# Order of the long and short products with standing weights in a hybrid layer, one Trainium2 core

## The chip, the core and the metric

The kernel runs on one core of one Trainium2 chip, in one launch. The metric is the device time of an execution in microseconds. The program was run three times: 1918.36, 1925.76 and 1926.24 us, so the median is 1925.76 us. Beside these times there is a profile of one execution, taken by the hardware profiler; all rows shown here are from it. Times in the timeline count from the first instruction of the profiled execution.

## The reference, cut to what matters

One layer of a network on 256 tokens of 2048 features, all in fp32. It has a dilated attention of three groups with 8 heads, a gated linear attention with 4 heads, a gated sum of the two branches, an output product, a layer norm, a feed-forward with a short convolution along the tokens, and a second layer norm. What fills the time are the products of the tokens with large weights:

```
parts = split(x @ w_in)            # 2048 x 19472
... attention on parts[:9] ...     # ya = attention @ w_proj_a   (1024 x 2048)
yb = (o * silu(gr)) @ w_proj_b     # 2048 x 2048
y  = sigmoid(m_a) * ya + sigmoid(m_b) * yb
x  = layernorm(ALPHA * x + y @ w_out)              # 2048 x 2048
g, u = x @ w_gate, x @ w_up                        # 2048 x 5632 each
x  = layernorm(ALPHA * x + (silu(conv(g)) * u) @ w_down)   # 5632 x 2048
```

## The kernel before

**Two parts of each number.** Every operand of the large products is split exactly into a main part and a rest of fewer bits each (`split`: ACT copies the number rounded into the main part, DVE subtracts it from the number and leaves the rest). A product is then the sum of main x main, main x rest and rest x main. For the tokens the two parts lie side by side in one tile of 512 columns: 256 tokens' main parts in the first half (`:S`), their rests in the second (`S:`).

**Pieces of weights.** All weights come as pieces of 128 x 2048 numbers, 1 MB each, in the order in which they are used. `piece` loads the next one (SP's queue, line 147), ACT makes the main part `whi` (line 115) and DVE the rest `wlo` (line 116). There are three buffers for the raw piece, two for `whi` and two for `wlo`.

**Two forms of product.** In the form that the diff touches the weights stand in TensorE's array and the tokens move past them; the result is 128 features by tokens. `b_tile` takes for each of 16 steps `kc` of 128 input features (8 steps for `yp`) a main part of the weights, 128 x 128, and moves all 512 columns past it (line 187: the long product), and then the rest of the weights and moves the 256 main columns past it, into the second half of the same bank (line 188: the short product). The first half of the bank then holds main x main, the second half the two mixed products; `b_sum` (lines 231 and 232, ACT and DVE) adds the halves. A bank is one tile of the pool `psm`, which has four.

In the other form (`a_chunk`, `a_part`, lines 237 to 239) the tokens stand and 512 columns of weights move: three products of 512 columns for each 128 tokens and step. It is used for `v`, `gv` and the product with `w_down` (`wd`), and the diff does not touch it.

**Where the touched form is used.** `b16` is `b_tile` with one piece and 16 steps. In order of time: `qk` (48 tiles, in four rounds with a head pair's attention beside them), `gqk` (16), `yp` (16 tiles of 8 steps), `gr` (16), `m` and `pb` (for each of 16 feature tiles two of `m` and one of `pb`), `wo` (16), and in the feed-forward `fg` and `fu` for 44 feature tiles in parts of 20, 20 and 4 (`FSPLIT`). After each part comes `wd`. The operand is `X` (the tokens) up to `m`, `YA` for `yp`, `OB` for `pb`, `YH` for `wo`, `X1` for the feed-forward. `OB` and `YH` are made feature tile by feature tile from the products just before: the last tile of `YH` comes from the last `pb` tile through ACT and DVE, and `wo`'s first tile reads it in its 16th step.

**Three tiles side by side.** The feed-forward's first three tiles (`fg` 0, `fu` 0, `fg` 1) are made by `b16_three` (lines 196 to 211) while DVE and ACT still make `X1` from the layer norm (lines 711 to 715): in each step a long and a short product for each of the three.

**What sets the order.** The kernel is written against a framework that plans each engine's order from dependencies and estimated costs, in the program's order where nothing speaks against it; small jobs of the attention are put into the stream of tiles from a list (`pump`). Each engine then runs its instructions strictly in the planned order. DVE and ACT thus make the split of a coming piece, the sums of a finished tile and the attention's steps one after the other. `piece_in_blocks` makes a piece out of turn, in small blocks.

Of the kernel before, what the change touches and what calls it, by code (L numbers as in the profile page):

```python
# [18 lines left out]
S = 256  # L19
# [13 lines left out]
ALPHA = 2.0 ** 0.25  # L33
# [3 lines left out]

# columns of w_in
C_GQ = 9216
# [6 lines left out]

# columns of the packed per-partition parameters
P_GB = 0
# [9 lines left out]
def hybrid_layer(ctx: ExitStack, tc: tile.TileContext, wp, xt, wgl, gw, par, relb, onehot, ln2, out):  # L58
    nc = tc.nc
# [10 lines left out]
    def act_set(name, after):  # L70
        """Load a set of ACT's tables once the instruction has been issued."""
        with tc.issue_after(after.ins):
            nc.scalar.preload_act_table_set(name)
# [5 lines left out]
    def blk(name, dt=F32):  # L79
        """2 KB of every partition."""  # L80
        n_blk[0] += 1
        return bpool.tile([P, 512], dt, tag="blk", name=f"{name}_{n_blk[0]}", bufs=NBLK)

    def tmp(name, dt=F32):
        """1 KB of every partition."""
        n_blk[0] += 1
        return tpool.tile([P, S], dt, tag="tmp", name=f"{name}_{n_blk[0]}", bufs=NTMP)

    def big(name, shape, dt=F32):
        """3 KB of every partition."""  # L90
        n_blk[0] += 1
        return tpool.tile([P, *shape], dt, tag="big", name=f"{name}_{n_blk[0]}", bufs=7)
# [17 lines left out]

# [1 line left out]
    n_piece = [0]  # L112
# [5 lines left out]
    def piece_in_blocks(i, on_pool=None):  # L118
        """A piece out of turn, or one that leaves the pool's parts to the next."""
        ws = []  # L120
        if on_pool is not None:
            raws = wpool.tile([P, 2048], F32, tag="raw", name=f"raw_{i}", bufs=3)
            nc.sync.dma_start(raws, wp[i])
        for c in range(4):
            cols = slice(c * 512, (c + 1) * 512)
            if on_pool is None:
                raw = blk("braw")
                nc.sync.dma_start(raw, wp[i, :, cols])
            else:
                raw = raws[:, cols]  # L130
            ws.append((blk("bhi", F32R), blk("blo", F32R)))
            split(*ws[-1], raw, nc.gpsimd if c in (on_pool or ()) else nc.vector)
        return ws

    def piece(before=(None,)):
        """Next piece, in as many cuts as there are entries of things to do before a cut."""
        i = n_piece[0]
        n_piece[0] += 1
        raw = wpool.tile([P, 2048], F32, tag="raw", name=f"raw_{i}", bufs=3)
        hi = wpool.tile([P, 2048], F32R, tag="whi", name=f"whi_{i}")  # L140
        lo = wpool.tile([P, 2048], F32R, tag="wlo", name=f"wlo_{i}")
        n = 2048 // len(before)
        for k, f in enumerate(before):
            if f is not None:
                f()
            c = slice(k * n, (k + 1) * n)
            nc.sync.dma_start(raw[:, c], wp[i, :, c])
            split(hi[:, c], lo[:, c], raw[:, c])
        return hi, lo

    side = []
# [9 lines left out]

# [1 line left out]
    def xtiles(name):  # L163
# [15 lines left out]

# [1 line left out]
    def b_tile(name, parts, opnd, nk):  # L181
        """[128 features, tokens]: main part in columns :S, the rest in S:."""
        ps = mbank(name)
        for kc in range(nk):
            hi, lo = parts(kc)
            xo = opnd(kc)
            nc.tensor.matmul(ps, hi, xo, start=(kc == 0), stop=False)  # L187
            nc.tensor.matmul(ps[:, S:], lo, xo[:, :S], start=False, stop=(kc == nk - 1))  # L188
        return ps
# [6 lines left out]
    def b16_three(names, opnd, second):  # L196
        """Three feature tiles side by side, for an operand that is still being made."""
        by_cols = lambda hi, lo: lambda kc: [a[:, kc * P : (kc + 1) * P] for a in (hi, lo)]
        ws = [by_cols(*piece((None,) * 4))]
        by_blk = lambda b: lambda kc: [a[:, (kc % 4) * P : (kc % 4 + 1) * P] for a in b[kc // 4]]  # L200
        ws.append(by_blk(second))
        ws.append(by_blk(piece_in_blocks(n_piece[0] + 1, (0, 1))))
        n_piece[0] += 2
        pss = [mbank(n) for n in names]
        for kc in range(16):
            xo = opnd(kc)
            for w, ps in zip(ws, pss):
                h, l = w(kc)
                nc.tensor.matmul(ps, h, xo, start=(kc == 0), stop=False)
                nc.tensor.matmul(ps[:, S:], l, xo[:, :S], start=False, stop=(kc == 15))  # L210
        return pss
# [4 lines left out]
    def evacuate(name, pss, parts=False):  # L216
        """[tile of tokens], or [tile of tokens][part]"""
        out = []
        for ps in pss:
            if parts:  # L220
                two = blk(name, F32R), blk(name, F32R)
                split(*two, ps)
                out.append(two)
            else:
                out.append(blk(name))
                nc.scalar.activation(out[-1], ps, AF.Copy)
        return out
# [13 lines left out]
    def a_chunk(name, opnd, nk, first=None, n_pump=1):  # L241
        """[128 tokens, 512] for both halves of the tokens."""
        pss = [mbank(f"{name}_t{t}") for t in range(2)]
# [10 lines left out]
    def a_pair_by_half(name, opnd, second):  # L254
        """Two chunks of one piece each: first all of one half of the tokens."""
        hi, lo = piece()
# [11 lines left out]

# [1 line left out]
    ident = cpool.tile([P, P], F32, name="ident")  # L270
# [14 lines left out]

# [1 line left out]
    bvs = dpool.tile([NH, 3, 384], F32, name="bvs")  # L287
# [16 lines left out]
    def copies():  # L304
        """Every row once for each of 32 queries, so that a row's start can move with the query."""
        nc.sync.dma_start(bvd, bvs[:, :, None, :].to_broadcast([NH, 3, 32, 384]))

    side.extend([lambda: None] * 4 + [distances(g) for g in range(3)] + [copies])

# [1 line left out]
    scale = HD ** -0.5  # L311
    YA = [None] * NH

    def attend(h, qk, vs, hp, hv):
        """Stages of head h: hp its place in its q and k tiles, hv in its v tiles."""
        st = {}
# [102 lines left out]

# [1 line left out]
    GK, GQ, GV = [], [], []  # L421
# [9 lines left out]

    # low-rank gate
    glr = tmp("glr")
# [3 lines left out]
    split(glh, gll, glr)  # L437
    # both operands of the gate's product three times over, from rows 0, 32 and 64, so that
    # one pass over the rows sums the products of their parts
    places = [slice(r, r + RANK) for r in (0, 32, 64)]  # L440
# [30 lines left out]
    def gla(h):  # L471
# [33 lines left out]
        def keys():  # L505
            q, k = GQ[h], GK[h]
            e1, e2, e3 = st["e1"], st["e2"], st["e3"]
            nc.vector.scalar_tensor_tensor(q, q, 256.0 ** -0.5, e1, op0=ALU.mult, op1=ALU.mult)
            # groups of two chunks of keys, for the chunks of queries 0 | 1 | 2, 3 | 2 | 3
            xk = [big("xk", (2, 3, 2, CH)) for _ in range(2)]  # L510
# [77 lines left out]

# [1 line left out]
    YP = []  # L590
# [12 lines left out]

# [1 line left out]
    OB = []  # L605
# [12 lines left out]

# [1 line left out]
    YH = []  # L620
# [21 lines left out]

# [1 line left out]
    act_set(ACT_LN_EXP, gated)  # L644
# [6 lines left out]
    def residual(d):  # L651
        """ALPHA x, less the centre."""
        if d % 2 == 0:
            R.append(blk("r"))
        xo = xop(d)
        r = r_of(d)
        nc.gpsimd.tensor_tensor(r, xo[:, :S].bitcast(F32), xo[:, S:].bitcast(F32), op=ALU.add)
        if d:
            nc.vector.scalar_tensor_tensor(r, r, ALPHA, cen, op0=ALU.mult, op1=ALU.subtract)
# [58 lines left out]

# [1 line left out]
    ACC = [[blk("acc") for _ in range(4)] for _ in range(2)]  # L720
# [12 lines left out]

# [1 line left out]
    G2, B2 = [], []  # L735
# [82 lines left out]

# [1 line left out]
def _by_rows(w, c, n):  # L820
    """Columns c..c+n of all rows, 128 rows to a partition's place."""
    k = w.shape[0] // P
# [45 lines left out]
def _bucket_rows():  # L868
    """One-hot buckets of the distance 255 - j, by group; a last row of -1e30 where it is masked."""
    out = np.zeros((NBUCKET + 1, 3, 384), np.float32)  # L870
# [61 lines left out]
```

## Time and profile before

| | |
|---|---|
| median of three runs | 1925.76 us (1918.36 to 1926.24) |
| profiled execution, span from first to last instruction | 1924.5 us |
| PE busy | 1897.7 us, 99% |
| weight loads (PEld) busy, beside PE | 1622.0 us, 84% |
| DVE busy | 1154.3 us, 60% |
| ACT busy | 900.1 us, 47% |
| POOL busy | 104.4 us, 5% |
| moved by DMA | 352.60 MB, mean 183 GB/s |

The span is 1.3 us below the median of the runs. PE stands for the products and PEld for the loads of their weights, which run beside products. The ends of products are modelled and products overlap, so the busy time of PE says that it was never long without work, and not that it worked at its peak. DVE, ACT and POOL are the vector, scalar and general engines, SP issues the transfers.

### The profile page before, as it was taken

Reading aid. Unit: us, or ns where it says so; the run is one execution under the profiler, and the core shown is the slowest. Engines: PE = TensorE matmul, PEld = TensorE weight load, DVE = VectorE, ACT = ScalarE, POOL = GpSimd, SP = SyncE. Lnnn points to the kernel's source line nnn. Section 1 sums busy time; section 2 is a strip of 40 time slices with the busy share of each in tenths; the row PEclk is TensorE's granted clock in tenths of the full one; section 3 lists DMA queues with packets and bytes.
Section 4 is the critical chain, followed back from the end, with each engine's and each line's share of the span. In section 5 each row is a group of like instructions: output and inputs, shape, how many; then the busy total and the mean of one; then the engine's idle time right before and its main releaser. Section 6 shows DMA issues by size and latency. Waiting matters only on the chain.

```text
span 1924.5 us, 24582 instructions
## 1 busy us (share of the span) xinstructions
PE 1897.7 (99%) x10208; PEld 1622.0 (84%) x10208; DVE 1154.3 (60%) x1324; ACT 900.1 (47%) x1084; POOL 104.4 (5%) x130
## 2 busy tenths in 40 slices
PE   9999999999999999999999998999999999999997
PEld 6888888888878888888888887888888888888885
DVE  5466565755656556655555757666654566664557
ACT  5445444453445554544444545554533455544342
POOL 0000000001000000000000452000000000000001
PEclk9999999999999999999999999999999999999998
DMA  7645545455544355555555553455555645555552
GB/s 273 231 178 175 191 175 182 166 191 175 180 154 145 140 191 182 194 178 195 177 193 179 197 192 114 176 190 182 190 186 195 239 180 192 181 191 200 198 194 86
DMA packets 56058, 352.60 MB, mean 183 GB/s; under 512 B 6737, under 2 KB 7660, under 8 KB 15500
## 3 DMA queue, kind: packets, MB, share of 16 engines
q1 hardware_dynamic: 53340, 345.10, 50.0%
q0 software_dynamic: 2464, 5.69, 1.0%
q8 instruction: 80, 1.31, 0.3%
q10 hardware_dynamic: 144, 0.26, 0.0%
q14 instruction: 30, 0.25, 0.0%
HBM read 348.85 MB, written 3.31 MB: 183 GB/s over the span
## 4 chain that ended last, share of the span: by engine, by line
PE 95%; DVE 3%; ACT 1%; issue 1%; DMA 1%; SPq 0%; DVEq 0%; ACTq 0%
PE qk L187 9%; PE fu L187 8%; PE fg L187 8%; PE m L187 6%; PE qk L188 5%; PE fu L188 4%; PE fg L188 4%; PE wd_t L238 4%; PE wd_t L237 4%; PE wd_t L239 4%; PE m L188 3%; PE pb L187 3%; PE gr L187 3%; PE gqk L187 3%; PE wo L187 2%; PE v_t L237 2%
## 5 line engine op out<-in xcount | busy, mean ns | idle before, releaser
L116 DVE TENSOR_TENSOR wlo<-raw,whi 128x2048 fp32r<-128x2048 f32 (+1 forms) x339 | 740.8, 2188 | 597.9 <-ACT whi L115 597.6
L115 ACT ACTIVATE whi<-raw 128x2048 fp32r<-128x2048 f32 (+1 forms) x339 | 617.4, 1824 | 454.7 <-issue 114.0
L187 PE MATMUL qk<-x,whi 128*128 128x512 f32 x768 | 273.8, 400 | 0.0
L187 PE MATMUL fu<-x,whi 128*128 128x512 f32 x688 | 244.9, 398 | 0.0
L187 PE MATMUL fg<-x,whi 128*128 128x512 f32 x672 | 239.7, 399 | 0.0
L188 PE MATMUL qk<-x,wlo 128*128 128x256 f32 x768 | 215.7, 281 | 0.0
L188 PE MATMUL fu<-x,wlo 128*128 128x256 f32 x688 | 193.2, 281 | 0.0
L188 PE MATMUL fg<-x,wlo 128*128 128x256 f32 x672 | 188.7, 281 | 0.0
L187 PE MATMUL m<-x,whi 128*128 128x512 f32 x512 | 181.7, 399 | 0.0
L187 PEld LDWEIGHTS qk<-x,whi 128*128 128x128 f32 x768 | 144.3, 188 | 35.3
L187 PEld LDWEIGHTS fu<-x,whi 128*128 128x128 f32 x688 | 129.2, 188 | 32.1
L187 PEld LDWEIGHTS fg<-x,whi 128*128 128x128 f32 x672 | 126.3, 188 | 31.0
L188 PEld LDWEIGHTS qk<-x,wlo 128*128 128x128 f32 x768 | 145.1, 189 | 0.0
L188 PE MATMUL m<-x,wlo 128*128 128x256 f32 x512 | 143.8, 281 | 0.0
L238 PE MATMUL wd_t<-wlo,h 128*128 128x512 f32 x344 | 134.1, 390 | 0.0
L239 PE MATMUL wd_t<-whi,h 128*128 128x512 f32 x344 | 133.9, 389 | 0.0
L237 PE MATMUL wd_t<-whi,h 128*128 128x512 f32 x344 | 133.7, 389 | 0.0
L188 PEld LDWEIGHTS fu<-x,wlo 128*128 128x128 f32 x688 | 130.0, 189 | 0.0
L188 PEld LDWEIGHTS fg<-x,wlo 128*128 128x128 f32 x672 | 127.0, 189 | 0.1
L187 PEld LDWEIGHTS m<-x,whi 128*128 128x128 f32 x512 | 96.2, 188 | 24.1
L188 PEld LDWEIGHTS m<-x,wlo 128*128 128x128 f32 x512 | 96.7, 189 | 0.0
L187 PE MATMUL pb<-ob,whi 128*128 128x512 f32 x256 | 91.1, 398 | 0.0
(251 smaller groups left out, 2991.5 us busy)
## 6 DMA issues: line engine op xcount, KB each, us to landing
raw<-in_wp SPq DMA_DIRECT2D x316, 1024.0 KB, 4.8
raw<-in_wp SPq DMA_DIRECT2D x24, 256.0 KB, 5.1
bias<-bvd POOLq DMA_DIRECT2D x32, 96.0 KB, 2.7
xraw<-in_xt SPq DMA_DIRECT2D x8, 256.0 KB, 5.2
braw<-in_wp SPq DMA_DIRECT2D x8, 256.0 KB, 5.0
ln<-in_ln POOLq DMA_DIRECT2D x8, 256.0 KB, 5.0
out<-acc SPq DMA_DIRECT2D x7, 256.0 KB, 2.5
bvd<-bvs SPq DMA_DIRECT2D x1, 1152.0 KB
```

The lines of the kernel that those rows point to most:

```text
L115: nc.scalar.activation(hi, src, AF.Copy)
L116: engine.tensor_tensor(lo, src, hi.bitcast(F32), op=ALU.subtract)
L187: nc.tensor.matmul(ps, hi, xo, start=(kc == 0), stop=False)
L188: nc.tensor.matmul(ps[:, S:], lo, xo[:, :S], start=False, stop=(kc == nk - 1))
L237: nc.tensor.matmul(ps, xh, hi, start=first, stop=False)
L238: nc.tensor.matmul(ps, xh, lo, start=False, stop=False)
L239: nc.tensor.matmul(ps, xl, hi, start=False, stop=last)
```

## The change

In `b_tile` the loop over the steps becomes two loops over the same steps: first all long products of the tile, then all short ones. The first product still opens the bank (`start`) and the last short one closes it (`stop`). In `b16_three` the loop over the steps issues the long products of the three tiles, and then come the 16 short ones of each tile in turn. Comments and docstrings are emptied as well, which changes no instruction.

```diff
     def b_tile(name, parts, opnd, nk):
         ps = mbank(name)
         for kc in range(nk):
-            hi, lo = parts(kc)
-            xo = opnd(kc)
-            nc.tensor.matmul(ps, hi, xo, start=(kc == 0), stop=False)
-            nc.tensor.matmul(ps[:, S:], lo, xo[:, :S], start=False, stop=(kc == nk - 1))
+            nc.tensor.matmul(ps, parts(kc)[0], opnd(kc), start=(kc == 0), stop=False)
+        for kc in range(nk):
+            nc.tensor.matmul(ps[:, S:], parts(kc)[1], opnd(kc)[:, :S], start=False, stop=(kc == nk - 1))
         return ps
...
         pss = [mbank(n) for n in names]
         for kc in range(16):
-            xo = opnd(kc)
             for w, ps in zip(ws, pss):
-                h, l = w(kc)
-                nc.tensor.matmul(ps, h, xo, start=(kc == 0), stop=False)
-                nc.tensor.matmul(ps[:, S:], l, xo[:, :S], start=False, stop=(kc == 15))
+                nc.tensor.matmul(ps, w(kc)[0], opnd(kc), start=(kc == 0), stop=False)
+        for w, ps in zip(ws, pss):
+            for kc in range(16):
+                nc.tensor.matmul(ps[:, S:], w(kc)[1], opnd(kc)[:, :S], start=False, stop=(kc == 15))
         return pss
```

## Rows read from the trace of the kernel before

**Rows 1.** Page: busy us (share of the span) by engine, and the chain's shares
```profile
PE 1897.7 (99%) x10208; PEld 1622.0 (84%) x10208; DVE 1154.3 (60%) x1324; ACT 900.1 (47%) x1084; POOL 104.4 (5%) x130
...
PE 95%; DVE 3%; ACT 1%; issue 1%; DMA 1%; SPq 0%; DVEq 0%; ACTq 0%
```
**Rows 2.** Groups by line, forms apart: count | busy us, mean ns | idle before
```profile
L187 PE MATMUL qk<-x,whi 128*128 128x512 f32 x768 | 273.8, 400 | 0.0
```
**Rows 3.** Timeline, PE, feed-forward: start us, duration us, line, product
```profile
1699.79 0.40 PE L187 MATMUL fg<-x,whi 128*128 128x512 f32 x1
1700.02 0.28 PE L188 MATMUL fg<-x,wlo 128*128 128x256 f32 x1
1700.14 0.40 PE L187 MATMUL fg<-x,whi 128*128 128x512 f32 x1
...
1700.50 0.40 PE L187 MATMUL fg<-x,whi 128*128 128x512 f32 x1
...
1705.44 0.40 PE L187 MATMUL fu<-x,whi 128*128 128x512 f32 x1
```
**Rows 4.** Timeline, PE: first products of gr, wo, second part's fg, wd
```profile
702.15 0.40 PE L187 MATMUL gr<-x,whi 128*128 128x512 f32 x1
...
1063.96 0.40 PE L187 MATMUL wo<-yh,whi 128*128 128x512 f32 x1
...
1507.59 0.39 PE L187 MATMUL fg<-x,whi 128*128 128x512 f32 x1
...
1733.71 0.40 PE L237 MATMUL wd_t<-whi,h 128*128 128x512 f32 x1
```
**Rows 5.** Timeline, PE, wd: a long product and the third one after it
```profile
1769.78 0.39 PE L237 MATMUL wd_t<-whi,h 128*128 128x512 f32 x1
...
1770.46 0.39 PE L237 MATMUL wd_t<-whi,h 128*128 128x512 f32 x1
```
**Rows 6.** Timeline, PE, wo: a long product and the 16th long after it
```profile
1077.55 0.39 PE L187 MATMUL wo<-yh,whi 128*128 128x512 f32 x1
...
1083.10 0.39 PE L187 MATMUL wo<-yh,whi 128*128 128x512 f32 x1
```
**Rows 7.** Timeline, PE and PEld, one of the attention's po products
```profile
211.87 0.28 PE L373 MATMUL po<-pT,v 128*128 128x256 f32 x1
211.87 0.19 PEld L374 LDWEIGHTS po<-pT,v 128*128 128x128 f32 x1
211.99 0.28 PE L374 MATMUL po<-pT,v 128*128 128x256 f32 x1
...
212.11 0.23 PE L375 MATMUL po<-pT,v 128*128 128x128 f32 x1
...
212.46 0.28 PE L188 MATMUL qk<-x,wlo 128*128 128x256 f32 x1
```
**Rows 8.** Tile po, PE: duration ns min/median/max, first and last start us
```profile
L374 PE MATMUL po<-pT,v x24: 279/282/285, 212.0 to 533.3; 128*128 128x256 f32 x24
```
**Rows 9.** Timeline, PE, wo near 1104; stretch: busy (x) per engine, PEclk, DMA, GB/s
```profile
1103.55 0.39 PE L187 MATMUL wo<-yh,whi 128*128 128x512 f32 x1
1106.40 0.41 PE L188 MATMUL wo<-yh,wlo 128*128 128x256 f32 x1 [2.46 <-DVE wlo L116]
...
1106.70:1110.00 3.30, 3.30 (x12) 2.82 (x12) 3.27 (x4) 0.42 (x1) 2.05 (x1) 0.50 0.72 253
```
**Rows 10.** Timeline, all engines, end of wo's first tile
```profile
1069.21 0.42 DVE L116 TENSOR_TENSOR yh<-y,yh 128x256 fp32r<-128x256 f32 x1
...
1070.14 0.40 PE L187 MATMUL wo<-yh,whi 128*128 128x512 f32 x1
```
**Rows 11.** Timeline, all engines, the three tiles side by side
```profile
1168.33 0.77 PE L209 MATMUL fg<-x,whi 128*128 128x512 f32 x1 [4.09 <-DVE x L715]
...
1179.91 1.26 DVE L715 SCALAR_TENSOR_TENSOR x<-r,prm,x 128x256 fp32r<-128x256 f32 x3
...
1186.39 0.28 PE L210 MATMUL fg<-x,blo 128*128 128x256 f32 x1
```

## The prediction

> **What bounds the kernel now.** I read the page's busy shares and its chain of waits first. The reader is to see that TensorE is busy for 1897.7 us of a 1924.5 us span and that 95% of the chain that ended last is PE [rows 1]. So every nanosecond that a product takes less time comes off the end, and what ACT, DVE and the DMA queues do counts only where PE waits for them.
>
> Next I read the groups by line. There are two kinds of product: a long one (line 187, 512 columns, weights `whi`) and a short one (line 188, 256 columns, weights `wlo`), 768 of each for `qk` alone. A long lasts 400 ns in the mean [rows 2], but that is not what it costs, because products overlap. The cost is the distance from one start to the next, and that is in the timeline. In the feed-forward the sequence runs long 1699.79, short 1700.02, long 1700.14, and the 17th long, which opens the next tile, is at 1705.44 [rows 3]: one tile of 16 pairs takes 5.65 us, a pair 353 ns. Two longer stretches agree: the 64 tiles of `gr`, `m` and `pb` take 1063.96 - 702.15 = 361.81 us, 5.653 each, and the 40 tiles of the second feed-forward part 1733.71 - 1507.59 = 226.12 us, 5.653 each [rows 4].
>
> Three more places price the same products in other surroundings.
> - In `wd` every product is long and each has its own weights: three take 1770.46 - 1769.78 = 0.68 us, 227 ns each [rows 5]. That is a long after a long.
> - In `wo` the same alternating pairs run at 5.55 us a tile (1083.10 - 1077.55), 347 ns a pair [rows 6]. The alternation has a quick and a slow form, 6.7 ns a pair apart.
> - In the attention's `po` a long product is followed by two of 256 columns and one of 128, each with weights of its own, and then by the next tile's pairs. The first short starts at 211.87, the second at 211.99, the third at 212.11, and the short of the next pair at 212.46 [rows 7]. Two shorts one behind the other: 120 ns. All four slots to 212.46 take 590 ns, which is 3 x 120 + 227 + 3, so even the 128-column one costs no more and no less than 120. The second short's weights begin to load as the first short starts (both at 211.87): the whole load lies beside one short product. Over 24 such places the second short's duration stays between 279 and 285 ns [rows 8].
>
> So 227 + 120 = 347 is the quick pair, and the slow pair has 6.7 ns more. I put those at the long that follows a short: its row reads 0.40 us in the slow tile and 0.39 in the quick one [rows 3, 6], while the short behind a short shows no such spread [rows 8].
>
> **The change part by part.** No product, load, byte or copy is added or removed. Only the order on PE changes: 16 longs, then 16 shorts.
>
> 1. *The slots.* A tile after the change has 15 longs behind a long, one long behind a short, 16 shorts: 16 x 226.7 + 16 x 120 + 7 = 5.554 us, against 5.653: 0.099 us less. Of the kernel's 237 tiles of 16 pairs (`yp`'s 16 half tiles counted as 8), I take as slow the 64 and 40 of [rows 4], the 8 of the last feed-forward part, 37 of the first, 48 `qk`, 8 `yp`, half of the 16 `gqk`: 213. 213 x 0.099 = 21.1 us. The 24 quick ones lose 0.007 each, and a few tiles of the first feed-forward part are quick too: in all -20.3 us. The bounds are from the price of a short in a run of 16, which no row shows beyond three: 120 ns [rows 7] and, at the dear end, 133, which is 120 and what the dearest slow pair has more than the quick one (1700.50 - 1700.14 = 360 against 347 ns [rows 3, 6]). I take 120, since the run of three is the nearest row.
>
> 2. *Waits of ACT and DVE for PE.* The last long of a tile comes 16 x 0.12 = 1.9 us earlier in its tile, so ACT may begin to overwrite `whi` for the piece after next that much sooner, and DVE's `wlo` is wanted only 16 x 0.227 = 3.6 us after a tile begins. Both add slack where PE hardly waits now, so I cost it at nothing. Evacuation (line 231) still waits for the last product of the bank; that comes no later relative to the tile's end.
>
> 3. *A wait that goes.* At 1103.55 a `wo` tile issued its first long and the short behind it waited 2.46 us for DVE's `wlo` [rows 9]. Then the granted clock was 0.50 from 1106.7 to 1110.0, the lower level of 1.2 GHz, after PE had stood still [rows 9]. With 16 longs in front, 3.6 us of work cover the wait: -2.5 us, and half of 3.3 us for the clock: -1.7. Late next is nothing in that tile.
>
> 4. *A wait that comes.* The first `wo` tile is the place where the operand is made just ahead of its use: the rest of `yh` for the 16th step is split by DVE from 1069.21 for 0.42 us, and the next tile's first long is at 1070.14 [rows 10]. Now that step comes at 15 x 353 ns = 5.3 us after 1063.96 and fits. Afterwards the 16th long is due at 1063.96 + 15 x 0.227 = 1067.4 and waits until 1069.63; behind it queue all 16 shorts. 1069.63 + 0.227 + 1.92 = 1071.8 against 1070.14: +1.6 us. If the clock falls behind this wait as it did in [rows 9], another 1.7.
>
> 5. *The three tiles side by side* (`b16_three`) start while DVE still makes `x1`: the first long at 1168.33, the last three parts of the operand from 1179.91 for 1.26 us, the last short at 1186.39 [rows 11]. Now the shorts fill the time between operands. Afterwards 48 longs go first at the operand's pace, and 48 x 0.12 = 5.76 us of shorts come behind: last operand 1181.17, three longs 0.68, shorts 5.76, so 1187.6 at the earliest and 1188.4 if PE is three operands behind. Against 1186.51: +1.1 to +1.9; I take +1.5.
>
> The sum: -20.3 - 4.2 + 1.6 + 1.5 = -21.4 us; 1924.5 - 21.4 = 1903.1 us of span. The median of the runs, 1925.76, lies 1.3 above that span, so 1904.
>
> The Trainium skill's "TensorE: Matmul & The Clock Gate", in the sections "Back-to-back issue gap" and "LDWEIGHTS (loading the stationary operand)", speaks against step 1: it gives a product N/2.4 + 2.5 ns (109 for 256 columns, 216 for 512) and a load of 128 columns 107 ns, so a load always hides and order would not matter; by it step 1 is zero. The trace doesn't agree in size: 227 ns where the page has 216 [rows 5], and an alternating pair that costs 353 in one place and 347 in another [rows 3, 6].
>
> **The rivals.**
> - *Order makes no difference.* The 6.7 ns may belong not to the change of kind but to whatever state PE is in over a long stretch (`wo` ran quick in the same order as `fg` [rows 3, 6]), and would then come back in the run of shorts, 126.7 ns each. For it: the two forms exist without any difference in the program. Against: the 24 tight durations [rows 8], measured amid slow tiles. Step 1 is then about +2 (the quick tiles join the slow), and the rest -1.1: 1925.
> - *The run of shorts is bound by its weight loads: slower.* In the old order every second load has a 227 ns product to lie beside; in the run each has 120. If the delay of a dear pair, 13 ns, falls on each short, a tile takes 16 x 226.7 + 16 x 133.3 = 5.76 us: +0.107 x 213 + 0.21 x 24 = +28 us, with the rest 1953. It decides from 126.7 ns a short upward. A load that could not overlap at all, 188 ns as PEld rows last, would give 16 x 0.068 = 1.1 us a tile; the second load at 211.87 with its product at 211.99 [rows 7] excludes that.
> - *The waits are dearer than I think.* The planner orders the engines anew; if a dozen tiles open a wait of 2 us as in step 4, the gain is gone. For it: step 4 itself. Against: everywhere else the operand is made long before. 1915 to 1925.
>
> **How the numbers follow.** My forecast has 0.64: 1904, by itself 1897 to 1912 (steps 3 to 5 at their ends, and the runs shown differ by 8 us). Order without effect 0.16, dearer waits 0.08, slower 0.12. Faster by over 0.5% (9.6 us, about what a measurement of this kernel can tell from no change) is 0.64 and half of the dear waits' case: 0.68. Within it: 0.16 and the other half, 0.20. Slower: 0.12. For 8 in 10 the range must take in the case without effect: 1896 to 1928.
>
> **What would show it.** In the timeline of the changed kernel a tile would be 16 longs 227 ns apart and then 16 shorts 120 apart, and a tile of the feed-forward 5.55 us. Shorts 127 apart mean the first rival, 130 and over the second. The 2.46 us wait of line 188's kind for `wlo` would be gone, a wait of PE for `yh` of some 2 us would stand in the first `wo` tile, and the three tiles side by side would end 1 to 2 us later after their start. If longs in a run are not 227 apart, or PE shows more than a handful of new waits of a microsecond, the prediction is wrong.

## The result and the profile after

The changed kernel takes 1904.99 us (median of four runs, 1903.91 to 1905.38). The kernel before, run beside it, has 1922.06 us (four runs, 1917.02 to 1926.24). The ratio is 0.9918, with a 95% interval of 0.9895 to 0.9941: faster, by 0.6 to 1.05%. The forecast was 1904, and later the same kernel had 1904.93 (four runs) against 1918.47 (seven runs of before on one chip, 1915.06 to 1923.57), ratio 0.9930 (0.9912 to 0.9948). So the time after the change met the forecast, and the gain, 17.1 us by the first medians and 13.5 by the second, is smaller than the 21 that the forecast took off. The runs of the changed kernel lie within 1.5 us, those of before within 11. That difference in spread belongs to the explanation.

On the page of the changed kernel (busy us by engine, then the chain that ended last) the reader is to see that nothing has changed places: PE still makes 95% of the chain, as in [rows 1]. The profiled execution's span is 1902.1 us, 22.4 below the one of before.

```profile
PE 1878.5 (99%) x10208; PEld 1625.5 (85%) x10208; DVE 1152.7 (61%) x1324; ACT 911.8 (48%) x1084; POOL 86.9 (5%) x130
...
PE 95%; DVE 3%; ACT 1%; issue 1%; DMA 0%; SPq 0%; DVEq 0%; ACTq 0%
```

The timeline of PE in the second feed-forward part answers to [rows 3] (start us, time from the first start to the last end, and how many neighbours a row joins). Line 185 is now the long product, line 187 the short one.

```profile
1489.78 3.79 PE L185 MATMUL fg<-x,whi 128*128 128x512 f32 x16
1493.40 2.08 PE L187 MATMUL fg<-x,wlo 128*128 128x256 f32 x16
1495.32 3.82 PE L185 MATMUL fu<-x,whi 128*128 128x512 f32 x16
1498.97 2.08 PE L187 MATMUL fu<-x,wlo 128*128 128x256 f32 x16
1500.88 1.32 PE L185 MATMUL fg<-x,whi 128*128 128x512 f32 x5
```

A tile takes 1500.88 - 1495.32 = 5.56 us where it took 5.65. The 16 shorts take 1.91 to 1.92 us, 120 ns each. The 16 longs of the first tile, which come behind the long products of `wd`, take 3.62 us, 226 each; those of the second tile, which come behind shorts, take 3.65.

By stages, from the first products of each (they answer to [rows 4] and to the end of `wo`):

```profile
695.98 0.40 PE L185 MATMUL gr<-x,whi 128*128 128x512 f32 x1
...
785.04 0.40 PE L185 MATMUL m<-x,whi 128*128 128x512 f32 x1
...
1142.29 0.38 PE L690 MATMUL pln<-s,ones 128*128 128x256 f32 x1
...
1712.42 0.40 PE L236 MATMUL wd_t<-whi,h 128*128 128x512 f32 x1
```

With `wo`'s first long at 1052.24 (below), `gr`, `m` and `pb` take 356.26 us for 64 tiles, 5.567 each, against 5.653; the 40 tiles of the second feed-forward part 1712.42 - 1489.78 = 222.64, 5.566 each. The `wo` stage, up to the product behind its last tile, takes 1142.29 - 1052.24 = 90.05 us against 93.80 (1157.76 - 1063.96, with this row of the kernel before):

```profile
1157.76 0.81 PE L691 MATMUL pln<-s,ones 128*128 128x256 f32 x3
```

The differences of all stages, before to after, in us:

| stage | difference | stage | difference |
|---|---|---|---|
| start to first `qk` | -1.67 | `wo` | -3.75 |
| `qk`, two halves | -4.33 | layer norm | -0.26 |
| `gqk` | -0.20 | three tiles and first feed-forward part | -2.05 |
| `yp` | -0.26 | second part | -3.48 |
| `gr` | -1.38 | third part | -0.70 |
| `m`, `pb` | -4.16 | tail | -0.40 |

The products in the other form (`v`, `gv`, `wd`) add 0.3. Of the start's 1.67, 1.03 lie before the first product of `v`, in the first transfers, which the change does not touch: the kernel before itself began `v` at 8.70, 8.85 and 7.65 us in its three profiles, the changed one at 7.67.

### The profile page after: what moved, and what is told of

The parts are those of the page before. It is cut to its first block, busy times and chain, and to the rows that moved or that the text cites. A ratio compares the mean times of both kernels' runs of the same rounds, so it can differ in the third digit from the quotient of the medians.

```text
span 1902.1 us, 24576 instructions
## 1 busy us (share of the span) xinstructions
PE 1878.5 (99%) x10208; PEld 1625.5 (85%) x10208; DVE 1152.7 (61%) x1324; ACT 911.8 (48%) x1084; POOL 86.9 (5%) x130
## 4 chain that ended last, share of the span: by engine, by line
PE 95%; DVE 3%; ACT 1%; issue 1%; DMA 0%; SPq 0%; DVEq 0%; ACTq 0%
PE qk L185 9%; PE fu L185 8%; PE fg L185 8%; PE m L185 6%; PE qk L187 5%; PE fu L187 4%; PE fg L187 4%; PE wd_t L236 4%; PE wd_t L238 4%; PE wd_t L237 4%; PE m L187 3%; PE gqk L185 3%; PE pb L185 3%; PE gr L185 3%; PE wo L185 3%; PE v_t L236 2%
## 5 line engine op out<-in xcount | busy, mean ns | idle before, releaser
L185 PE MATMUL qk<-x,whi 128*128 128x512 f32 x768 | 184.2, 392 | 0.0
L185 PE MATMUL fu<-x,whi 128*128 128x512 f32 x688 | 164.1, 391 | 0.0
L185 PE MATMUL fg<-x,whi 128*128 128x512 f32 x672 | 160.7, 391 | 0.0
L185 PE MATMUL m<-x,whi 128*128 128x512 f32 x512 | 122.1, 391 | 0.0
L187 PE MATMUL qk<-x,wlo 128*128 128x256 f32 x768 | 99.6, 283 | 0.0
L187 PE MATMUL fu<-x,wlo 128*128 128x256 f32 x688 | 89.3, 283 | 0.0
L187 PE MATMUL fg<-x,wlo 128*128 128x256 f32 x672 | 87.2, 283 | 0.0
L236 PE MATMUL v_t<-whi,x 128*128 128x512 f32 x192 | 75.8, 397 | 0.6 <-ACT whi L115 0.6
L238 PEld LDWEIGHTS wd_t<-whi,h 128*128 128x128 f32 x344 | 64.6, 188 | 13.5
L237 PEld LDWEIGHTS wd_t<-wlo,h 128*128 128x128 f32 x344 | 64.6, 188 | 13.4
```

Of the source, the lines that this page charges most:

```text
L185: nc.tensor.matmul(ps, parts(kc)[0], opnd(kc), start=(kc == 0), stop=False)
L187: nc.tensor.matmul(ps[:, S:], parts(kc)[1], opnd(kc)[:, :S], start=False, stop=(kc == nk - 1))
L236: nc.tensor.matmul(ps, xh, hi, start=first, stop=False)
L237: nc.tensor.matmul(ps, xh, lo, start=False, stop=False)
L238: nc.tensor.matmul(ps, xl, hi, start=False, stop=last)
```

## The experiments

Theory A: a long product behind a short one costs more, and the change takes such places away. Theory B: the old order has a slow and a quick form by itself, and only strict alternation has them. Several kernels tell these and the causes behind them apart. Tile times are worked out from the 48 tiles of `m` and `pb` unless it is said otherwise, and the bare time of a tile, 16 x 226.7 + 16 x 120, is 5.547 us.

**The kernel of before, again, twice.** No edit.

> The kernel of before once more, unchanged. Its runs lie at 1917 to 1918 and at 1926 us. Theory S, quick and slow alternation is settled anew in each execution at small disturbances: an execution near 1918 has some 60 to 80 more quick tiles (7 to 8 us / 0.107) than the 24 of the profiled one, and one near 1926 about as many. Rival: the spread has another place (the start, transfers, the tail), and the number of quick tiles is 24 whatever the time.

It took 1918.90 us, span 1917.1. The timeline of its PE shows the first products of `gr` and `wo`:

```profile
701.52 0.39 PE L187 MATMUL gr<-x,whi 128*128 128x512 f32 x1
...
1056.50 0.39 PE L187 MATMUL wo<-yh,whi 128*128 128x512 f32 x1
```

The 64 tiles between take 354.98 us, 5.547 each: here all of `gr`, `m` and `pb` ran in the quick form that [rows 6] show for `wo`, and the first profiled execution had them slow (361.81 us in [rows 4]). That is 6.83 us; `yp` adds 0.63. The spans differ by 7.38. All other stages agree to 0.2 us. So what separates these two executions is quick and slow alternation, in the same program. Theory S held for them; that the whole spread of the kernel before has this cause is likely, and not shown beyond the executions that were profiled.

> The kernel of before a third time under the profile. The first profiled execution (span 1924.5) ran gr, m and pb slow at 5.653 us a tile, the second (1917.1) quick at 5.547, and their other stages agree to 0.1 us but for yp. If quick and slow are drawn anew in each execution, some stage of this one differs again from both by a multiple of about 0.107 us a tile, and the stages' differences add up to the difference of the spans. If gr, m and pb alone can switch, the span is near 1924 or near 1917.

1918.10 us, span 1916.4, and `gr` to `wo` again 354.99 us:

```profile
700.50 0.39 PE L187 MATMUL gr<-x,whi 128*128 128x512 f32 x1
...
1055.49 0.39 PE L187 MATMUL wo<-yh,whi 128*128 128x512 f32 x1
```

`qk` and the feed-forward parts are slow in all three executions, and the second and third part agree to 10 ns. But `wo` switched. After its wait for `wlo`, which here is 1.8 us and not 2.5, its tiles run in the slow form, where [rows 6] and the second execution have the quick one. A long product of `wo` and the 16th long after it:

```profile
1125.24 0.40 PE L187 MATMUL wo<-yh,whi 128*128 128x512 f32 x1
...
1130.89 0.40 PE L187 MATMUL wo<-yh,whi 128*128 128x512 f32 x1
```

That is 5.65 us. The shorter wait hides it in the stage's sum (94.13 us against 93.80 and 93.94). So a new draw was seen in two places, from `yp` to `pb` and in `wo`, and not everywhere. In the three profiles a form, once entered, lasts until other products or a wait break the alternation (`gr`, `m` and `pb` are of one form for 355 to 362 us); one switch, at 668 us of the first profile, came without such a break.

**Groups.** In `b_tile`, with n of 2, 4 and 8:

```diff
-        for kc in range(nk):
-            ... long
-        for kc in range(nk):
-            ... short
+        for k0 in range(0, nk, n):
+            for kc in range(k0, k0 + n):
+                ... long
+            for kc in range(k0, k0 + n):
+                ... short
```

> Two longs, then their two shorts, and so on through a tile (the changed kernel otherwise). Theory A, the extra time is paid at each change from short to long: the changed kernel pays some 20 ns at its one change per tile, spread over the first five longs (236, 236, 229, 232, 231 against 227), and two longs in a row pay the first two of these, some 18 ns less 7 that the shorts behind give back: 8 changes x 11 = 88 ns, so 5.63 us a tile and about 1922 us in all. Theory B, the extra time belongs to strict alternation alone and any other order is free of it: 5.55 to 5.57 us a tile, about 1905 us. Between them, a price of 6.7 ns for each change: 5.60 us, about 1913 us.

> Four longs, then their four shorts. Theory A (a change from short to long costs some 18 ns over the four longs behind it): 4 x 18 = 73 ns, 5.62 us a tile, about 1919 us. Theory B (alternation alone is slow): 5.55 to 5.57 us, about 1905 us. A fixed 6.7 ns for each change: 5.574 us, about 1906 us.

> Eight longs, then their eight shorts. Groups of four paid 66 ns a tile over the bare 5.547 us (16.6 a change), the changed kernel 19 (one change), groups of two 26 (3.3 a change). If a change from short to long costs 17 to 19 ns wherever four or more shorts stand before it: 2 x 19 = 38 ns, 5.585 us a tile, about 1909 us. If the price grows with the run of shorts, it lies nearer to 5.60.

Measured, in one run each: 1909.04, 1915.70 and 1909.71 us. The first products of `m` and `wo` in the kernels with groups of two, four and eight:

```profile
786.15 0.40 PE L186 MATMUL m<-x,whi 128*128 128x512 f32 x1
...
1053.67 0.40 PE L186 MATMUL wo<-yh,whi 128*128 128x512 f32 x1
```
```profile
789.63 0.40 PE L186 MATMUL m<-x,whi 128*128 128x512 f32 x1
...
1059.07 0.40 PE L186 MATMUL wo<-yh,whi 128*128 128x512 f32 x1
```
```profile
786.44 0.40 PE L186 MATMUL m<-x,whi 128*128 128x512 f32 x1
...
1054.60 0.40 PE L186 MATMUL wo<-yh,whi 128*128 128x512 f32 x1
```

Divided by 48: 5.573, 5.613 and 5.587 us, so 26, 66 and 40 ns over the bare tile, or 3.3, 16.6 and 20 ns for each change from short to long. The changed kernel with one change has 20. Theory A's price holds from groups of four upward (66 against 73 expected, 40 against 38) and fails for groups of two (26 against 88), where theory B nearly holds; theory B fails for four. More changes are not always worse: the price of one depends on the length of the runs, and the quick alternation, with a change at each pair, pays nothing (5.547 us).

**The size of the short product.** In the alternating kernel of before (and, for the second, in the changed one):

```diff
-            nc.tensor.matmul(ps[:, S:], lo, xo[:, :S], ...)
+            nc.tensor.matmul(ps[:, 256:448], lo, xo[:, :192], ...)   # alt192, and in run192
+            nc.tensor.matmul(ps[:, 192:512], lo, xo[:, :320], ...)   # alt320
+            nc.tensor.matmul(ps, lo, xo, ...)                        # alt512
```

> The kernel of before, alternating, with shorts of 320 columns (64 more than wanted, so the sums are others). Free of any extra a pair is 226.7 + 320 / 2.4 + 13.3 = 373.3 ns, 5.97 us a tile. If the extra of slow pairs is the long's wait for its load, the longer cover takes it away: 5.97 us in all tiles, about 2000 us. If it is a price of changing between the kinds of product, slow pairs stay: 380 ns, 6.08 us a tile, about 2025 us.

2024.83 us. The first products of `m` and `wo`:

```profile
828.83 0.40 PE L187 MATMUL m<-x,whi 128*128 128x512 f32 x1
...
1120.66 0.40 PE L187 MATMUL wo<-yh,whi 128*128 128x512 f32 x1
```

291.83 / 48 = 6.08 us, 380 ns a pair, and the second feed-forward part has (1828.79 - 1585.61) / 40 = 6.08 too. With 27 ns more cover for the next load an extra of 6.7 ns a pair is still there. So it is not a long that waits for its weights. Every pair takes 380 ns here (the starts are 233 and 147 apart), where the slow form of before went through 350, 360 and 350; that it is the same extra is taken from its size alone.

> The kernel of before, alternating, with shorts of all 512 columns into the whole bank (main and rest parts of the tokens both: more than wanted). All products then have one shape, and only the weights change between main part and rest. If the extra of a slow pair comes from the change of shape, it is gone: 2 x 226.7 = 453.3 ns a pair, 7.25 us a tile, about 2303 us. If it comes from the change between the two tiles of weights: 460 ns, 7.36 us a tile, about 2327 us.

2305.08 us, and 348.17 / 48 = 7.253 us a tile, 453.3 ns a pair, with nothing over. The stretch of `m` and `pb` could have been quick by itself, as it was in two profiles of before. So the second feed-forward part, slow in all three of them, is the better witness: (2100.02 - 1809.88) / 40 is 7.253 as well. The rows are the first products of `m`, `wo`, the second part's `fg` and `wd`:

```profile
935.62 0.39 PE L187 MATMUL m<-x,whi 128*128 128x512 f32 x1
...
1283.79 0.39 PE L187 MATMUL wo<-yh,whi 128*128 128x512 f32 x1
...
1809.88 0.39 PE L187 MATMUL fg<-x,whi 128*128 128x512 f32 x1
...
2100.02 0.39 PE L237 MATMUL wd_t<-whi,h 128*128 128x512 f32 x1
```

The weights still change between `whi` and `wlo` at each product. With one shape for all products the extra is gone, so it needs the change of shape. (What changes with the columns here is also the place in the bank, the second half or the whole of it; no run takes the two apart.) The change alone is not enough, since the quick form changes shape as often and has no extra.

> The changed kernel with shorts of 192 columns (64 tokens' share of main times rest is left out). If a short in a run is bound by its weights' load, which has only the short before it to lie beside, the slot stays near the 120 ns that 256 columns take, and not below the 109 to 112 ns at which the transposes and the attention's 64-column products follow one another: 5.38 to 5.57 us a tile, 1862 to 1905 us. If it is bound by its columns: 93 ns, 5.14 us a tile, about 1803 us.

1876.70 us. A tile of `gr` in the timeline of PE:

```profile
762.19 1.92 PE L187 MATMUL gr<-x,wlo 128*128 128x192 f32 x16
763.96 3.83 PE L185 MATMUL gr<-x,whi 128*128 128x512 f32 x16
```

Sixteen shorts of 192 columns take 763.96 - 762.19 = 1.77 us, 110.6 ns each, and not 93. The first of them, behind a long, takes 86 and the others 111.8 in the mean of 226 tiles. The transposes of 128 columns in the kernel before stand 108 to 110 ns apart (`pback`) and products of 64 columns 111 to 112 (`patt`). From 64 to 192 columns the distance hardly follows the columns, so it is put down to the load of the new weights that each of them has: some 109 to 112 ns. At 256 columns, 120 ns, the columns are the bound, by 8 ns.

> The kernel of before, alternating, but each short of the tiles moves 192 columns (64 tokens' share of main times rest is left out). If the long behind a short waits for the load of its weights, which lies beside the short, a pair gains nothing from the shorter stream: 227 + 120 to 127 = 347 to 353 ns, 5.55 to 5.65 us a tile, 1903 to 1925 us. If the short's own columns set its slot (192 / 2.4 + 13.3 = 93.3 ns), a pair takes 320 to 327 ns, 5.12 to 5.23 us a tile, about 1800 to 1825 us.

1961.90 us, outside what either theory gave. The pair itself is near what the first one says, 344 ns (950.39 to 950.73):

```profile
950.04 0.42 PE L187 MATMUL m<-x,whi 128*128 128x512 f32 x1
950.30 0.25 PE L188 MATMUL m<-x,wlo 128*128 128x192 f32 x1
950.39 0.42 PE L187 MATMUL m<-x,whi 128*128 128x512 f32 x1
...
950.73 0.41 PE L187 MATMUL m<-x,whi 128*128 128x512 f32 x1
```

A fourth less in each short bought at most 9 ns of the 27 that the columns gave up. The loss comes with waits that the expectation had no place for; the two largest groups of PE's new waits (total us, times, longest):

```profile
PE fu L188 <- DVE wlo L116: 28.8, 38, 1.8
PE gr L188 <- DVE wlo L116: 6.7, 12, 0.7
```

Nearly every `fu` tile's first short waited for DVE's split. Here that split is planned later against its tile than in the kernel before, where no such wait is found; why the plan moved was not tried.

**The three tiles side by side as before.**

```diff
         for kc in range(16):
             for w, ps in zip(ws, pss):
-                ... long
-        for w, ps in zip(ws, pss):
-            for kc in range(16):
-                ... short
+                ... long
+                ... short
```

> The changed kernel, but the three tiles side by side alternate as before. In the changed kernel the time from their first long to the first long of the next tile and on to the end of the first feed-forward part fell by 2.05 us, where 37 tiles x 0.087 would give 3.2 less what some quick tiles take back. The prediction's step 5 says that the reordered three cost 1.1 to 1.9 us: this kernel then gains that, 1903.5 us. The rival, that transposes for the second residual filled PE's gaps and only 0.6 us was lost: 1904.4 us, and the stretch from the first long of the three to the first product of wd is 0.4 to 0.8 us shorter than the changed kernel's 228.35.

1905.97 us, a single run against the changed kernel's 1903.9 to 1905.4. From the first long of the three to the first product of `wd` it takes 1383.02 - 1154.15 = 228.87 us; the changed kernel takes 1380.95 - 1152.60 = 228.35. Undoing this part thus looks 0.5 us slower, where both theories had it gain. But the two stretches did not have the same clock. From the first long of the three to the first long of the next tile, in the kernels before, changed and undone (us, busy by engine with counts, then the granted clock):

```profile
1168.33:1186.86 18.53, 18.53 (x100) 16.18 (x101) 15.14 (x29) 14.81 (x31) 3.06 (x4) 0.92 0.00 1
```
```profile
1152.60:1172.85 20.25, 20.02 (x109) 17.13 (x110) 17.78 (x32) 16.50 (x33) 3.06 (x4) 0.93 0.06 20
```
```profile
1154.15:1173.79 19.64, 19.64 (x101) 17.13 (x101) 15.14 (x29) 14.81 (x31) 3.06 (x4) 0.86 0.06 10
```

The undone kernel has the order of before and took 1.1 us more for it, at 0.86 instead of 0.92. Behind the wait for the operand the clock was at its lower level, 1.2 GHz, and stayed there longer: 4.6 us after the first long a long still lasted 0.63 us, where the kernel before had 0.40 again after 3.3 us. So this run does not show that the new order gains. At nearly equal clock, before against changed, the three tiles end 20.25 - 18.53 = 1.72 us later after their start, and in them PE made nine transposes more. PE of the changed kernel:

```profile
1156.07 0.49 PE L727 MATMUL pback<-ident,r 128*128 128x128 f32 x3
1156.79 0.50 PE L206 MATMUL fg<-x,whi 128*128 128x512 f32 x1 [0.23 <-DVE x L714]
...
1161.39 0.71 PE L727 MATMUL pback<-ident,r 128*128 128x128 f32 x5
```

While the operand is awaited, the planner lets PE transpose for the second residual (line 727: 13 transposes in four places, two of them shown; the kernel before had 4 there and the rest behind the three tiles). Nine transposes at 109 ns are 1.0 us of the 1.72, so the new order itself cost an estimated 0.7 us, near the rival's 0.6. The one wait left inside is 0.23 us.

**Two tiles to a run.** Neighbouring tiles share 32 longs and 32 shorts:

```diff
+        pss = [mbank(name) for _ in two]
+        for ps, parts in zip(pss, two):
+            for kc in range(nk):
+                ... long
+        for ps, parts in zip(pss, two):
+            for kc in range(nk):
+                ... short
```

> Two neighbouring tiles share their runs: 32 longs, then 32 shorts, for qk, gqk, gr, the two m of a feature tile, fg with fu, and yp's half tiles (106 pairs of tiles). If a change from short to long costs the same 19 ns however long the run before it, each pair of tiles saves one: 106 x 19 = 2.0 us, 1903 us against the changed kernel's 1905. The rival: with both pieces' parts held at once ACT and DVE are late with the next two, PE waits, and the kernel is slower than the changed one: above 1907 us, with PE idle in front of line 187's kind of product.

> The changed kernel once more, unchanged, beside the others of this call. Its own runs lie at 1903.9 to 1905.4: if the two forms of the pair are gone with the alternation it stays within 1903 to 1906; if its runs of longs and shorts had forms of their own, some execution would lie 5 us or more away.

1905.10 us (four runs, 1904.17 to 1906.29) against 1904.93 (1904.46 to 1905.29) for the changed kernel beside it: no difference. Inside, the theory's saving is there (`m` and `pb` 1052.35 - 785.47 = 266.88 us against 267.20, which is 16 changes x 20 ns; the second feed-forward part 222.24 against 222.64), 1.4 us in all stages of this form, but the first two `wd` stages took 0.3 us more each and the third, with the tail, 0.6. And no run of the changed kernel lies away from the others: its eight runs lie between 1903.91 and 1905.38, and the spread is gone with the alternation.

## Why the prediction was right

**The bound and the mechanism.** PE was the bound and stayed it, and the time came from the slots: the stages of this form, the three tiles included, give 16.6 of the 22.4 us. Shorts in a run take 120 ns, as the nearest row had it [rows 7], and longs in a run 227 [rows 5].

**Step 1, the term of the sum that was mis-sized.** It was put at 0.099 us a tile and measured 0.087 (5.653 to 5.566), and its total at 20.3 where the stages show 16.6 with the three tiles, some 17.3 without the 0.7 that these cost (below). The 7 ns for one long behind a short were too few: a change from 16 shorts to longs costs 20 ns. Over 149 tiles of the changed kernel's `gr`, `m`, `pb`, `fg` and `fu` the mean distances behind the first five longs are 236, 236, 229, 232 and 231 ns and then 227, while the first short behind a long takes 114. The price is spread over several products, which no row of alternating pairs could show. But the trace before had it elsewhere. Where the three shorter products of `po` are followed by the longs of `v`:

```profile
218.36 0.23 PE L375 MATMUL po<-pT,v 128*128 128x128 f32 x1
218.42 0.45 PE L237 MATMUL v_t<-whi,x 128*128 128x512 f32 x1
218.71 0.40 PE L238 MATMUL v_t<-wlo,x 128*128 128x512 f32 x1
218.94 0.39 PE L239 MATMUL v_t<-whi,x 128*128 128x512 f32 x1
219.17 0.40 PE L237 MATMUL v_t<-whi,x 128*128 128x512 f32 x1
```

By the trace's starts in ns the distances behind the second to the fifth long are 236, 229, 232 and 231, then 227: the same series. The 128-column product and the first long take 348 together. The prediction split this sum at [rows 7] into 120 and 227 and read from it that the 128-column product costs no less than 120; the rows do not fix the split, and with the 112 ns of the runs of 192 columns the long has an estimated 236, the first number of the series. The quick tiles also lose more than it said: the new tile, 5.566 us, is 0.020 dearer than the quick form's 5.547, and not 0.007.

**The cause behind step 1.** The prediction charged the extra to the long behind a short and left open whether its load was to blame. The kernel with longer shorts speaks against the load, the one with equal shapes shows that the extra needs the change of shape. What in the engine takes five products to settle, and what selects the quick or slow form of the alternation, stays open; the profiles show only that the form changes where the alternation is broken, at most such places in the same way in all three executions of the kernel before.

The Trainium skill's "TensorE: Matmul & The Clock Gate", section "LDWEIGHTS (loading the stationary operand)", has P / 1.2 ns for a load of P columns, by an estimate 107 ns for 128; the run of 192-column shorts, 111.8 ns apart behind its first, agrees with it to 5 ns. The section "Back-to-back issue gap" of the same page has N / 2.4 + 2.5 ns for a product by itself, by an estimate 109 and 216 ns for 256 and 512 columns, and about 131 ns for 512 columns in a stream; here they take 120 and 227 in a stream, and it has no term for a change of shape, so by it the order would not have mattered. The measurement decides.

**Step 2** held: `wo` apart, no new wait of PE of more than 0.5 us appeared.

**Step 3** held. No product of `wo` waits for `wlo` any more, and the clock stays at the upper level: the stretch of the stage (us, busy by engine with counts, then the granted clock) reads 1.00, where [rows 9] had 0.50 behind the wait.

```profile
1052.20:1142.30 90.10, 89.94 (x517) 79.13 (x516) 65.87 (x78) 40.77 (x48) 33.04 (x36) 1.00 0.55 192
```

The stage lost 3.75 us, against 4.2 less the 1.6 that step 4 was to cost.

**Step 4** failed. It said that the 16 shorts queue behind the 16th long and 1.6 us are lost. PE at that place:

```profile
1052.24 5.40 PE L185 MATMUL wo<-yh,whi 128*128 128x512 f32 x23
1057.81 0.50 PE L185 MATMUL wo<-yh,whi 128*128 128x512 f32 x1 [0.17 <-DVE yh L116]
1058.15 2.07 PE L187 MATMUL wo<-yh,wlo 128*128 128x256 f32 x16
```

The first row joins 23 longs, not 15: in the program's order on PE, 8 longs of the second tile stand between the 15th and the 16th of the first. The planner put them into the wait; 0.17 us were left. The operand itself came at nearly the same time after the tile's start as before: DVE's split of `yh` began 5.09 us after it, against 5.25. The trace before had shown this filling, and the prediction misread it when it said that the 16th step fits. Between 1063.96 and 1070.14 stand 17 pairs and not 16, and only the last comes behind the split's end at 1069.63:

```profile
1069.26 0.40 PE L187 MATMUL wo<-yh,whi 128*128 128x512 f32 x1
...
1069.69 0.50 PE L187 MATMUL wo<-yh,whi 128*128 128x512 f32 x1
```

The 16th step is thus the pair at 1069.69, and one pair of the second tile already stood in front of it.

**Step 5** was too dear for the same reason. It charged 1.5 us; the three tiles do end 1.7 us later after their start, as it said, but 1.0 of that is transposes that PE no longer has to make afterwards, and some 0.7 us are left.

**The two errors and the rest.** Steps 1 and 5 together were put at -18.8 us and gave -16.6; steps 3 and 4 at -2.6 and gave -3.75; the start, the layer norm and the tail, left out of the sum, gave 2.3, and the other form of product took 0.3 back. So the predicted span of 1903.1 met 1902.1, partly by errors that cancel: that is luck, and so is much of the start's 1.67 us, since the kernel before comes to its first `qk` at 76.77, 76.66 and 75.70 us in its own three profiles.

**The rivals.** "Order makes no difference" had seen rightly that the same order runs in a quick and a slow form: with the quick form in `gr` to `pb` the kernel before took 1918.90 and 1918.10 us, and against these the change is worth 13 to 14 us and not 21. But the extra did not come back in the runs of shorts. (Its 1925 is a span; taken to the runs' median like the other forecasts it is 1926.7.) "Bound by its weight loads" missed by 8 ns: the load's pace is some 112 ns and the short takes 120. "Dearer waits" did not appear in this kernel; in the one with shorter shorts a shifted plan opened 28.8 us of waits in `fu` alone.

## What to carry to other kernels

Where a stream of products with new weights each is bound by TensorE, price a product by the distance of starts in each surrounding that the trace has, and look for the same code running at two speeds: an order that mixes shapes may have more than one steady form, and two executions then differ for no other reason. Put equal shapes in long runs where the alternation runs slow, but do not expect it to beat the quick form: here 5.567 us a tile stood between 5.547 and 5.653, and groups of four, 5.613, were worse than groups of two or sixteen. Making all shapes equal took the extra away as well, but its added columns cost far more than that (2305 us). Before charging a moved step with a wait, look in the trace for what the planner already puts into such gaps. Before reading a difference of half a microsecond between two kernels, compare the granted clock in the stretch.

## What the runs showed of the hardware that was not expected

Alternating products of 512 and 256 columns ran in two steady forms, 346.7 and 353.3 ns a pair, in the same stage of the same program in different executions, and a form lasted for more than 350 us. In the quick form a change of shape costs nothing over 226.7 + 120; with two products of each kind in turn a change from short to long cost 3.3 ns, with four 16.6, with eight and with sixteen 20. Products of 512 columns that alternate between two tiles of weights cost 226.7 ns each, with nothing over, and products of 192 columns in a run stood 111.8 ns apart, where their columns alone would give an estimated 93.
